# A decoder layer's down projection: four plain passes over the width, or seven of eight by Strassen's scheme

## The chip, the cores and the metric

One core of a Trainium2 chip runs the kernel once. The metric is the device time of one execution in microseconds (us); several executions give a median. The engines of the core are called by the profile's names: PE (TensorE, matmuls), PEld (its weight loads, which overlap the matmuls), DVE (VectorE), ACT (ScalarE), POOL (GpSimd) and SP (SyncE, which here issues nearly all DMAs).

## The reference

The layer has S = 512 tokens of width D = 1024; all data are float32. In short:

```python
a = rmsnorm(x, g_mix_pre);  z = a @ w_in
mix = concat(pool_mixer(z), moba_attention(z)) @ w_out
h = x + rmsnorm(mix, g_mix_post)
m = rmsnorm(h, g_mlp_pre)
f = square(relu(m @ w_up)) @ w_down          # w_up 1024x4096, w_down 4096x1024
h = h + rmsnorm(f, g_mlp_post)
out = h + sigmoid(h @ w_ple_gate) * (p @ w_ple_proj)
```

## The kernel before

Every product is made in three passes: each operand is split into a high part (rounded to the matmul's format by an ACT cast, line 123) and a low remainder (a DVE subtraction, line 124), and `three` (lines 158 to 160) multiplies high by high, high by low and low by high into one PSUM bank. A bank holds 128 rows of 512 columns; the program names eight: three `one`, three `four`, two `tp`.

Weights come in units of 128 x 1024 numbers (512 KB). `load` takes the next unit of a fixed list as soon as one of six slots is free: a DMA on SP into one of three `raw` buffers, the ACT cast, the DVE subtraction. `done` frees a slot behind the last matmul that reads it, so the list runs some five units ahead of PE. A planner puts each engine's instructions in an order ahead of the run, by program order and its own estimate of times; at run time each engine keeps that order.

The stages are: norm of x and the products with `w_in` and `w_ple_proj` (`embed(0, ...)` keeps the first half of the embedding's product in the tile `pp`); attention and pooling, head by head; the output projection in two halves `o0`, `o1` with both norms (`normed`), the second half of the embedding (`embed(1, ...)`) and the transposes of the normed rows (`mlp_rows`); the MLP; the gate.

The MLP goes over the 4096 in four chunks of 1024. In a chunk, `up` makes eight groups of 128 features for all 512 tokens (24 matmuls each), followed by relu (ACT), square (DVE), cast (ACT) and subtraction (DVE). The down products `tokens("d...")` take the two halves of the 1024 outputs in turn: the four token tiles fill four banks, and at a chunk's end ACT or DVE adds them to `facc` in SBUF. The last chunk goes half by half and tile by tile, with the norm's steps (lines 665 to 674), a transpose (`to_features`, line 238) and split of each finished tile behind its matmuls. The gate (lines 689 to 692) follows, tile by tile, in two halves.

The factor 2^-10 (`DOWN`) holds the rows that go into the MLP in range, whatever the gains; `squares` later takes it back out.

Of the kernel before, what the change touches and what calls it, by code (L numbers as in the profile page):

```python
# [25 lines left out]
NCH = 4  # L26
LINE = 512
FILL_LEFT, FILL_RIGHT = 192, 480
DOWN = 2.0 ** -10
# [13 lines left out]
def hybrid_layer(ctx: ExitStack, tc: tile.TileContext, x, p, w_in, w_pool, pool_scale, w_out,  # L43
# [68 lines left out]
    for c in range(NCH):  # L112
        for f in range(FC):
            rows(f"u{c}_{f}", w_up, 0, ND, (c * FC + f) * P, P)
        for hf in range(2):
            rows(f"d{c}_{hf}", w_down, c * FC, FC, hf * HALF, 512)
    for hf in range(2):
        rows(f"s{hf}", w_ple_gate, 0, ND, hf * HALF, 512)
# [10 lines left out]
    def load():  # L129
        while free and nxt[0] < len(units):  # L130
            i = nxt[0]
            nxt[0] += 1
            pool, s = free.pop(0)
            src, n, _ = units[i]
            raw = wts.tile([P, UD], F32, tag="raw", bufs=RAW, name="raw")
            hi = pool.tile([P, UD], F32R, tag=f"wh{s}", bufs=1, name=f"wh{s}")
            lo = pool.tile([P, UD], F32R, tag=f"wl{s}", bufs=1, name=f"wl{s}")
# [107 lines left out]
    pp = [keep.tile([P, NT, HALF], F32, name="pp0")]  # L245
    pT_h = keep.tile([P, NPK, S], F32R, name="pT_h")
    pT_l = keep.tile([P, NPK, S], F32R, name="pT_l")
# [43 lines left out]

    for t in range(NT):
        ms = small.tile([P, 1], F32, name="ms")
        an = begin.tile([P, D], F32, tag="an", bufs=2, name="an")
        with tc.issue_after(p_split.ins):
            mean_square(ms, xs[t], an)
        r = rstd(ms, eps)
        for hf in range(2):
            c = slice(hf * HALF, (hf + 1) * HALF)
            nc.vector.scalar_tensor_tensor(an[:, c], xs[t][:, c], r, gpre[:, c],  # L300
                                           op0=ALU.mult, op1=ALU.mult)
            to_features(an[:, c], aT_h, aT_l, t, 4 * hf, 4 * hf + 4)

    def embed(hf, bank, ts):
        for t in ts:
            o = bank()
            marks = tokens(f"e{hf}", pT_h, pT_l, [t], [o], t == NT - 1)
            (nc.scalar.copy if hf else nc.vector.tensor_copy)(pp[hf][:, t, :], o)
        return marks[-1]
# [224 lines left out]
    pp.append(mlp.tile([P, NT, HALF], F32, name="pp1"))  # L534
# [5 lines left out]
    def junk(n):  # L540
        return mlp.tile([P, n], F32, tag="rq", bufs=4, name="junk")
# [16 lines left out]

    def normed(t, o):
# [7 lines left out]
        for c in (LO, HI):  # L567
            last = nc.vector.scalar_tensor_tensor(m[:, c], h[:, c], DOWN, gmlp[:, c],
                                                  op0=ALU.mult, op1=ALU.mult)
# [29 lines left out]

    ypool.release()  # L600
    late = ctx.enter_context(tc.tile_pool(name="late", bufs=1, side="right", reuse_waits="tile"))
    fs = [small.tile([P, 2], F32, name="fs") for _ in ts]

    def up(c, f, fh, fl, cols=slice(0, S), last=True):
        n = cols.stop - cols.start
        o = one()[:, :n]
        mm = features(f"u{c}_{f}", mT_h, mT_l, o, cols, last)
        r = mlp.tile([P, n], F32, tag="rq", bufs=4, name="r")
        q = mlp.tile([P, n], F32, tag="rq", bufs=4, name="q")
# [5 lines left out]
    squares = []  # L615
    for c in range(NCH):
        if c == 1:
            table(AF.Sigmoid, facc[:, 0, 0:1])
        fh = late.tile([P, FC, S], F32R, tag="fh", bufs=1, name="fh")
        fl = late.tile([P, FC, S], F32R, tag="fl", bufs=1, name="fl")  # L620
        ahead = AHEAD if c == 0 else 0
        for f in range(ahead):
            mm = up(c, f, fh, fl, slice(0, S // 2), False)
            if f == 0:
                with tc.high_priority(), tc.issue_after(mm):
                    mlp_rows(NT - 1)
                mid.release()
                end = ctx.enter_context(tc.tile_pool(name="end", bufs=1, reuse_waits="tile"))
                facc = end.tile([P, NT, D], F32, name="facc")
                gfin = spread(end, g_mlp_post, "gfin")  # L630
        for f in range(FC):
            up(c, f, fh, fl, slice(S // 2 if f < ahead else 0, S))
        if c == 0:
            for t in ts:
                ms = small.tile([P, 2], F32, name="ms2")
                for hf, cc in enumerate((LO, HI)):
                    with tc.issue_after(root):
                        mean_square(ms[:, hf:hf + 1], h_sb[:, t, cc], junk(HALF))
                with tc.issue_after(made_m):
                    nc.vector.tensor_scalar(ms[:, 1:2], ms[:, 1:2], EPS, None, op0=ALU.add)  # L640
                    r = rstd(ms[:, 0:1], ms[:, 1:2])
                    q = small.tile([P, 2], F32, name="r2", bufs=NT)
                    nc.vector.tensor_scalar(q[:, 0:1], r, r, DOWN ** -2, op0=ALU.mult, op1=ALU.mult)
                    nc.vector.tensor_scalar(q[:, 1:2], q[:, 0:1], isd, None, op0=ALU.mult)
                squares.append(q)
        for hf in range(2):
            cc = slice(hf * HALF, (hf + 1) * HALF)
            if c < NCH - 1:
                os = [four(), four(), four(), one()]
                tokens(f"d{c}_{hf}", fh, fl, ts, os, True)  # L650
                for t in ts:
                    if c == 0:
                        nc.scalar.copy(facc[:, t, cc], os[t])
                    else:
                        nc.vector.tensor_add(facc[:, t, cc], facc[:, t, cc], os[t])
                continue
            if hf == 0:
                hT_h = act.tile([P, ND, S], F32R, tag="aTh", name="hT_h")
                hT_l = act.tile([P, ND, S], F32R, tag="aTl", name="hT_l")
            for t in ts:  # L660
                o = four()
                tokens(f"d{c}_{hf}", fh, fl, [t], [o], t == NT - 1)
                with tc.high_priority():
                    d, h = facc[:, t, :], h_sb[:, t, :]
                    nc.vector.tensor_add(d[:, cc], d[:, cc], o)
                    mean_square(fs[t][:, hf:hf + 1], d[:, cc], junk(HALF), squares[t][:, 1:2])
                    nc.vector.tensor_mul(d[:, cc], d[:, cc], gfin[:, cc])
                    if hf == 0:
                        nc.vector.tensor_scalar(fs[t][:, 0:1], fs[t][:, 0:1], EPS, None, op0=ALU.add)
                        continue  # L670
                    r = rstd(fs[t][:, 1:2], fs[t][:, 0:1], squares[t][:, 0:1])
                    for b in range(2):
                        bb = slice(b * HALF, (b + 1) * HALF)
                        nc.vector.scalar_tensor_tensor(h[:, bb], d[:, bb], r, h[:, bb],
                                                       op0=ALU.mult, op1=ALU.add)
                        to_features(h[:, bb], hT_h, hT_l, t, 4 * b, 4 * b + 4)
# [3 lines left out]
    for hf in range(2):  # L680
        for t in ts:
            tail = hf == 1 and t == NT - 1
            for c0, n in ((0, HALF // 2), (HALF // 2, HALF // 2)) if tail else ((0, HALF),):
                cc = slice(hf * HALF + c0, hf * HALF + c0 + n)
                o = four()[:, :n]
                tokens(f"s{hf}", hT_h, hT_l, [t], [o], t == NT - 1 and c0 + n == HALF,
                       slice(c0, c0 + n))
                g = mlp.tile([P, n], F32, tag="rq", bufs=4, name="g")
                nc.scalar.activation(g, o, AF.Sigmoid)
                nc.vector.tensor_mul(g, g, pp[hf][:, t, c0:c0 + n])  # L690
                nc.vector.tensor_add(g, g, h_sb[:, t, cc])
                nc.sync.dma_start(ot[t][:, cc], g)

# [28 lines left out]
```

## Time and profile before

| what | value |
|---|---|
| median of 3 executions (lowest, highest) | 602.88 us (602.8, 603.0) |
| the profiled execution's own time | 602.55 us |
| its span, first to last instruction | 600.8 us |
| busy: PE, DVE, ACT, POOL | 589.4, 320.3, 258.3, 53.3 us |
| granted clock of PE over the span | 0.999 |

Busy time counts the union of an engine's instructions. A matmul's end is modelled, so its listed length (0.39 us) is longer than the distance between two of them.

### The profile page before, as it was taken

Reading aid. Unit: us, or ns where it says so; the run is one execution under the profiler, and the core shown is the slowest. Engines: PE = TensorE matmul, PEld = TensorE weight load, DVE = VectorE, ACT = ScalarE, POOL = GpSimd, SP = SyncE. Lnnn points to the kernel's source line nnn. Section 1 sums busy time; section 2 is a strip of 40 time slices with the busy share of each in tenths; the row PEclk is TensorE's granted clock in tenths of the full one; section 3 lists DMA queues with packets and bytes.
Section 4 is the critical chain, followed back from the end, with each engine's and each line's share of the span. In section 5 each row is a group of like instructions: output and inputs, shape, how many; then the busy total and the mean of one; then the engine's idle time right before and its main releaser. Section 6 shows DMA issues by size and latency. Waiting matters only on the chain.

```text
span 600.8 us, 7438 instructions
## 1 busy us (share of the span) xinstructions
PE 589.4 (98%) x2854; PEld 492.5 (82%) x2854; DVE 320.3 (53%) x594; ACT 258.3 (43%) x447; POOL 53.3 (9%) x92
## 2 busy tenths in 40 slices
PE   8999999999999999999999999999999999999997
PEld 5678998987778998888888888888888888888886
DVE  5832788996558754622245334444244444368632
ACT  6554857676534544642434221343212343246221
POOL 2327363221000000000000000000000000000000
PEclk9999999999999999999999999999999999999999
DMA  8706431321390543233332233323323333043111
GB/s 313 218 16 175 116 109 57 97 79 36 93 328 1 174 141 106 73 107 100 106 105 90 86 106 105 95 83 104 105 76 102 104 106 103 3 140 99 43 54 52
DMA packets 65636, 63.16 MB, mean 105 GB/s; under 512 B 2356, under 2 KB 48184, under 8 KB 65600
## 3 DMA queue, kind: packets, MB, share of 16 engines
q1 hardware_dynamic: 65312, 61.90, 32.9%
q10 hardware_dynamic: 288, 0.79, 0.4%
q8 instruction: 22, 0.36, 0.2%
q14 instruction: 14, 0.11, 0.1%
HBM read 60.56 MB, written 2.12 MB: 104 GB/s over the span
## 4 chain that ended last, share of the span: by engine, by line
PE 88%; DVE 4%; ACT 3%; DMA 2%; issue 1%; POOL 0%; SPq 0%; ACTq 0%
PE ps_one L159 15%; PE ps_one L158 15%; PE ps_one L160 15%; PE ps_four L158 13%; PE ps_four L159 13%; PE ps_four L160 13%; ACT wh L123 1%; PE ps_tp L481 1%; PE ps_tp L238 1%; DMA raw<-in_w_ple_proj_dram 1%; PE ps_one L495 1%; DMA raw<-in_w_up_dram 1%; PE ps_one L496 1%; DVE wl L124 1%; PE ps_four L455 1%
## 5 line engine op out<-in xcount | busy, mean ns | idle before, releaser
L124 DVE TENSOR_TENSOR wl<-raw,wh 128x1024 fp32r<-128x1024 f32 (+1 forms) x87 | 105.1, 1211 | 163.0 <-ACT wh L123 162.4
L123 ACT CAST wh<-raw 128x1024 fp32r<-128x1024 f32 (+1 forms) x99 | 103.0, 1043 | 177.5 <-PE ps_one L160 79.0
L159 PE MATMUL ps_one<-mT_l,wh 128*128 128x512 f32 (+1 forms) x280 | 104.0, 372 | 0.4 <-DVE mT_l L124 0.4
L158 PE MATMUL ps_one<-mT_h,wh 128*128 128x512 f32 (+1 forms) x280 | 103.5, 371 | 0.0
L160 PE MATMUL ps_one<-mT_h,wl 128*128 128x512 f32 (+1 forms) x280 | 103.5, 371 | 0.0
L160 PE MATMUL ps_four<-wh,fl 128*128 128x512 f32 x208 | 81.0, 389 | 0.0
L158 PE MATMUL ps_four<-wh,fh 128*128 128x512 f32 x208 | 81.0, 389 | 0.0
L159 PE MATMUL ps_four<-wl,fh 128*128 128x512 f32 x208 | 80.9, 389 | 0.0
L159 PEld LDWEIGHTS ps_one<-mT_l,wh 128*128 128x128 f32 x280 | 52.7, 188 | 9.6 <-DVE mT_l L124 0.6
L158 PEld LDWEIGHTS ps_one<-mT_h,wh 128*128 128x128 f32 x280 | 52.6, 188 | 9.2
L160 PEld LDWEIGHTS ps_one<-mT_h,wl 128*128 128x128 f32 x280 | 52.6, 188 | 9.0
L158 PEld LDWEIGHTS ps_four<-wh,fh 128*128 128x128 f32 x208 | 39.0, 188 | 8.1
L160 PEld LDWEIGHTS ps_four<-wh,fl 128*128 128x128 f32 x208 | 39.0, 188 | 8.1
L159 PEld LDWEIGHTS ps_four<-wl,fh 128*128 128x128 f32 x208 | 39.0, 188 | 8.0
L158 PE MATMUL ps_one<-aT_h,wh 128*128 128x512 f32 (+1 forms) x120 | 42.3, 352 | 0.2 <-ACT ks L443 0.2
L160 PE MATMUL ps_one<-aT_h,wl 128*128 128x512 f32 (+1 forms) x120 | 41.9, 351 | 0.0
L159 PE MATMUL ps_one<-aT_l,wh 128*128 128x512 f32 (+1 forms) x120 | 41.9, 349 | 0.0
L123 ACT CAST fh<-q 128x512 fp32r<-128x512 f32 (+1 forms) x35 | 20.4, 583 | 41.9 <-DVE q L611 41.9
L124 DVE TENSOR_TENSOR fl<-q,fh 128x512 fp32r<-128x512 f32 (+1 forms) x35 | 22.6, 645 | 20.0 <-ACT fh L123 19.7
L124 POOL TENSOR_TENSOR wl<-raw,wh 128x1024 fp32r<-128x1024 f32 x12 | 28.7, 2400 | 29.7 <-ACT wh L123 29.6
L158 PE MATMUL ps_four<-wh,hT_h 128*128 128x512 f32 (+1 forms) x72 | 26.4, 367 | 0.0
L160 PE MATMUL ps_four<-wh,hT_l 128*128 128x512 f32 (+1 forms) x72 | 26.4, 368 | 0.0
(187 smaller groups left out, 934.7 us busy)
## 6 DMA issues: line engine op xcount, KB each, us to landing
raw<-in_w_up_dram SPq DMA_DIRECT2D x32, 512.0 KB, 3.8
raw<-in_w_down_dram SPq DMA_DIRECT2D x32, 512.0 KB, 3.7
raw<-in_w_in_dram SPq DMA_DIRECT2D x16, 512.0 KB, 4.1
raw<-in_w_out_dram SPq DMA_DIRECT2D x8, 512.0 KB, 3.7
raw<-in_w_ple_gate_dram SPq DMA_DIRECT2D x8, 512.0 KB, 4.6
T<-lines SPq DMA_DIRECT2D x8, 256.0 KB, 3.4
h_sb<-in_x_dram SPq DMA_DIRECT2D x4, 512.0 KB, 8.2
out_dram<-g SPq DMA_DIRECT2D x7, 256.0 KB, 2.0
```

The lines of the kernel that those rows point to most:

```text
L123: nc.scalar.copy(dst_hi, src)
L124: return (lo or nc.vector).tensor_tensor(dst_lo, src, f32(dst_hi), op=ALU.subtract)
L158: nc.tensor.matmul(o, sh, mh, start=start, stop=False)
L159: nc.tensor.matmul(o, sh, ml, start=False, stop=False)
L160: return nc.tensor.matmul(o, sl, mh, start=False, stop=stop)
L238: turned = nc.tensor.transpose(tp[:, k, :], src[:, (b - b0 + k) * P:(b - b0 + k + 1) * P], ident)
L455: nc.tensor.matmul(o[:, :wide], q[:, c], lo[:, :wide], start=False, stop=True)
L481: nc.tensor.transpose(tp[:, k, :], probs[t][:, k * P:(k + 1) * P], ident)
L495: nc.tensor.matmul(o[:, q0:], v, ph[:, c], start=k == 0, stop=False)
L496: nc.tensor.matmul(o[:, q0:], v, pl[:, c], start=False, stop=k == NT - 1)
```

## The change

The width is cut into eight chunks of 512 instead of four of 1024. In chunks 0 to 6 the down product of a chunk, 512 tokens by 512 features by 1024 outputs, is done by Strassen's scheme in Winograd's form: tokens, features and outputs are halved, and seven products of 256 x 256 x 512 take the place of eight. The seven stand in the order 1, 2, 6, 5, 7, 3, 4, with the next chunk's four `up` groups between them. Sums of the activations' quarters (`rows_of`: s1, s2, s3 and a fourth written over s2) and of the weights' quarters (`weights_of`: t1, t2, and two written in place) are DVE operations; each of the seven activations' and weights' operands is split into high and low. Products 2 and 4 stay in four PSUM banks over all seven chunks; the other five go through the two `tp` banks and are added in SBUF (`acc`) each chunk. At the end of chunk 6 five pairs of `acc` are combined (`add`). The weights' quarters are loaded whole (`fetch`, 512 KB each) and wait in `late`. The square of `up` moves from DVE to ACT, and the split of the hidden values moves to the quarters.

Chunk 7 is plain, and goes by token tiles with both halves of the outputs in turn; tiles 2 and 3 are transposed inside the gate's first matmuls (`turned_rows`).

The embedding's product goes to DRAM (`ppd`) through two small buffers and comes back before the gate. The factor 2^-10 becomes a factor per row worked out early from x and `g_mix_post` (`scale_of`, `size`); the table load ahead of chunk 1 is gone, and the scratch tiles `rq` have three buffers instead of four.

```diff
-NCH = 4
+NCH = 8
...
+            if callable(src):
+                src(hi, lo)
...
+            pp = keep.tile([P, HALF], F32, tag="pp", bufs=2, name="pp")
+            (nc.scalar.copy if hf else nc.vector.tensor_copy)(pp, o)
+            nc.sync.dma_start(ppd[hf, t], pp)
...
+    for hf, c in enumerate((LO, HI)):
+        mean_square(sq[:, hf:hf + 1], gpost[:, c], junk(HALF))
+    nc.vector.tensor_scalar(size, msx, sq[:, 0:1], sq[:, 1:2], op0=ALU.add, op1=ALU.add)
+    nc.scalar.activation(size, size, AF.Sqrt, bias=eps)
+    nc.vector.reciprocal(scale_of, size)
...
+    def weights_of(m, c):
+        def make(hi, lo):
+            b = {n: quads.get((n, c)) for n in ("11", "12", "21", "22")}
...
+            elif m == 6:
...
+                less(t1, b["12"], b["11"])
+                fetch("11", c + 1)
+                less(src, b["22"], t1)
+                fetch("21", c + 1)
...
+            elif m == 7:
+                src = b["12"]
+                less(src, b["22"], src)
...
+                src = b["21"]
+                less(src, src, quads["t2"])
+            split(hi, lo, flat(src))
+            if m in (7, 3):
+                fetch("12" if m == 7 else "22", c + 1)
...
+    order = [1, 2, "u0", 6, 5, "u1", 7, "u2", 3, "u3", 4]
...
         nc.scalar.activation(r, o, AF.Relu)
-        nc.vector.tensor_mul(q, r, r)
-        split(fh[:, f, cols], fl[:, f, cols], q)
+        nc.scalar.activation(qs_of[c][:, f, cols], r, AF.Square)
...
+        if m == 6:
+            nc.vector.tensor_add(tile("s1"), a["21"], a["22"])
+            less(tile("s2"), sums["s1"], a["11"])
+        elif m == 7:
+            less(tile("s3"), a["11"], a["21"])
+        elif m == 3:
+            less(sums["s2"], a["12"], sums["s2"])
...
+        split(hi, lo, src)
...
+    def product(m, c, i, o, start, stop):
...
+        for n in range(PAIRS):
+            three(o, sh[:, n, k], sl[:, n, k], wh[:, n, :], wl[:, n, :], start and n == 0,
+                  stop and n == PAIRS - 1)
...
+    held = {2: [four(), four()], 4: [four(), one()]}
+    def products(m, c):
+        for i in range(2):
+            if m in held:
+                product(m, c, i, held[m][i], c == 0, False)
+            else:
+                o = bank()
+                product(m, c, i, o, True, True)
+                if c == 0:
+                    nc.scalar.copy(acc[m][:, i, :], o)
+                else:
+                    nc.vector.tensor_add(acc[m][:, i, :], acc[m][:, i, :], o)
...
+    for c in range(NCH - 1):
+        for m in order:
+            if isinstance(m, str):
+                up(c + 1, int(m[1]))
                 continue
+            if k < len(line_up):
+                rows_of(*line_up[k])
+                k += 1
+            products(m, c)
...
+    for n in range(2 * NT):
+        nc.sync.dma_start(pp[n], ppd[n // NT, n % NT])
+    for t in ts:
+        mm = last_rows(t)
+        if t >= 2:
+            turned_rows(t - 2, mm)
...
+                if hf == 0 and t in (1, 2):
+                    turned_rows(t + 1, marks[1])
```

## Rows read from the trace of the kernel before

**Rows 1.** The page's first part and its chain: busy time of each engine, shares.

```profile
PE 589.4 (98%) x2854; PEld 492.5 (82%) x2854; DVE 320.3 (53%) x594; ACT 258.3 (43%) x447; POOL 53.3 (9%) x92
...
PE 88%; DVE 4%; ACT 3%; DMA 2%; issue 1%; POOL 0%; SPq 0%; ACTq 0%
```

**Rows 2.** Busy time by stretch: start, attention, before the MLP, steady MLP, end.

```profile
core 0: us, PE busy (x) PEld busy (x) DVE busy (x) ACT busy (x) POOL busy (x), PEclk, DMA share, GB/s
0.00:30.00 30.00, 25.73 (x105) 17.83 (x106) 21.73 (x47) 17.31 (x28) 8.52 (x44) 1.00 0.82 265
90.00:120.00 30.00, 29.81 (x184) 26.52 (x183) 27.03 (x72) 21.87 (x52) 9.43 (x16) 1.00 0.24 77
190.00:217.00 27.00, 26.60 (x198) 25.02 (x197) 19.82 (x33) 16.09 (x29) 0.00 (x0) 1.00 0.42 128
250.00:500.00 250.00, 250.00 (x1105) 207.01 (x1104) 98.61 (x133) 80.79 (x110) 0.00 (x0) 1.00 0.32 97
541.00:601.00 60.00, 55.52 (x284) 47.01 (x282) 32.06 (x55) 18.77 (x30) 0.00 (x0) 0.99 0.18 62
```

**Rows 3.** Groups by shape: line, engine, operation, count, busy, mean ns, idle before.

```profile
L124 DVE TENSOR_TENSOR wl<-raw,wh 128x1024 fp32r<-128x1024 f32 x85 | 103.8, 1224 | 157.7 <-ACT wh L123 157.1
L123 ACT CAST wh<-raw 128x1024 fp32r<-128x1024 f32 x97 | 101.8, 1052 | 174.4 <-PE ps_one L160 79.0 <-PE ps_one L159 67.5 <-PE ps_four L160 13.5
...
L158 PE MATMUL ps_four<-wh,fh 128*128 128x512 f32 x208 | 81.0, 389 | 0.0
...
L124 DVE TENSOR_TENSOR fl<-q,fh 128x512 fp32r<-128x512 f32 x29 | 20.1, 692 | 19.4 <-ACT fh L123 19.3
L611 DVE TENSOR_TENSOR q<-r 128x512 f32<-128x512 f32 x29 | 19.8, 684 | 0.0
...
L158 PE MATMUL ps_one<-wh,fh 128*128 128x512 f32 x48 | 18.7, 389 | 0.0
...
L123 ACT CAST fh<-q 128x512 fp32r<-128x512 f32 x29 | 18.0, 621 | 39.2 <-DVE q L611 39.2
L610 ACT ACTIVATE r<-ps_one 128x512 f32<-128x512 f32 x29 | 17.1, 591 | 0.0
...
L655 DVE TENSOR_TENSOR facc<-facc,ps_four 128x512 f32<-128x512 f32 x12 | 7.9, 682 | 2.3 <-PE ps_four L160 2.3
```

**Rows 4.** Timeline of DVE and ACT ahead of the MLP: start us, us, what.

```profile
189.54 1.28 DVE L124 TENSOR_TENSOR mT_l<-ps_tp,mT_h 128x512 fp32r<-128x512 f32 x2
...
198.01 3.48 DVE L124 TENSOR_TENSOR wl<-raw,wh 128x1024 fp32r<-128x1024 f32 x3
...
191.90 2.94 ACT L123 CAST wh<-raw 128x1024 fp32r<-128x1024 f32 x3
194.75 1.54 ACT L308 COPY pp<-ps_one 128x512 f32<-128x512 f32 x3
196.18 1.08 ACT L123 CAST mT_h<-ps_tp 128x512 fp32r<-128x512 f32 x2
```

**Rows 5.** Who waited for whom: total us, times, longest us.

```profile
DVE wl L124 <- ACT wh L123: 162.4, 66, 4.9
```

**Rows 6.** Timeline at a bank's release: DVE behind PE, PE behind DVE.

```profile
544.10 0.39 PE L160 MATMUL ps_four<-wh,fl 128*128 128x512 f32 x1
...
544.53 0.69 DVE L665 TENSOR_TENSOR facc<-facc,ps_four 128x512 f32<-128x512 f32 x1 [0.31 <-PE ps_four L160]
...
172.67 0.68 DVE L551 TENSOR_TENSOR mg<-ps_four,gpost 128x512 f32<-128x512 f32 x1
...
173.40 0.50 PE L158 MATMUL ps_four<-wh,Yh 128*128 128x512 f32 x1 [0.66 <-DVE ms L550]
```

**Rows 7.** Timeline of DVE and of SP's queue, 14 to 19 us.

```profile
14.18 1.28 DVE L308 COPY pp<-ps_four 128x512 f32<-128x512 f32 x2
15.38 1.22 DVE L124 TENSOR_TENSOR wl<-raw,wh 128x1024 fp32r<-128x1024 f32 x1
...
16.62 2.23 SPq L143 DMA_DIRECT2D raw<-in_w_in_dram  x2
```

**Rows 8.** DMA issues: count, KB each, median us from issue to landing.

```profile
h_sb<-in_x_dram SPq DMA_DIRECT2D x4, 512.0 KB, 8.2
out_dram<-g SPq DMA_DIRECT2D x7, 256.0 KB, 2.0
```

More of the change, by code (lines that the diff above doesn't have):

```diff
@@ L111, in hybrid_layer @@
     rows("e1", w_ple_proj, 0, NPK, HALF, 512)
[L112 to L118, printed above, removed]
+    for f in range(FC):
+        rows(f"u0_{f}", w_up, 0, ND, f * P, P)
     by_pool = set(range(groups["q0"][0], groups["o0"][0]))
@@ L134, in load @@
             src, n, _ = units[i]
+            if s == "q":
+                both = pool.tile([P, 2, UD], F32R, tag="q", bufs=2, name="wq")
+                hi, lo = both[:, 0], both[:, 1]
+            else:
+                hi = pool.tile([P, UD], F32R, tag=f"wh{s}", bufs=1, name=f"wh{s}")
+                lo = pool.tile([P, UD], F32R, tag=f"wl{s}", bufs=1, name=f"wl{s}")
+            if callable(src):
+                src(hi, lo)
+                loaded[i] = [t.rearrange("q (k c) -> q k c", k=n) for t in (hi, lo)] + [(pool, s)]
+                continue
             raw = wts.tile([P, UD], F32, tag="raw", bufs=RAW, name="raw")
-            hi = pool.tile([P, UD], F32R, tag=f"wh{s}", bufs=1, name=f"wh{s}")
-            lo = pool.tile([P, UD], F32R, tag=f"wl{s}", bufs=1, name=f"wl{s}")
             raw_k = raw.rearrange("q (k c) -> q k c", k=n)
@@ L244, in hybrid_layer @@
     keep = ctx.enter_context(tc.tile_pool(name="keep", bufs=1))
-    pp = [keep.tile([P, NT, HALF], F32, name="pp0")]
-    pT_h = keep.tile([P, NPK, S], F32R, name="pT_h")
-    pT_l = keep.tile([P, NPK, S], F32R, name="pT_l")
+    ppd = tc.dram_tile([2, NT, P, HALF], F32, name="ppd")
+    ppool = tc.alloc_tile_pool(name="ppool", bufs=1, side="right", reuse_waits="tile")
+    pT_h = ppool.tile([P, NPK, S], F32R, name="pT_h")
+    pT_l = ppool.tile([P, NPK, S], F32R, name="pT_l")
     aT_h = act.tile([P, ND, S], F32R, tag="aTh", name="aT_h")
@@ L290, in hybrid_layer @@
             nc.sync.dma_start(xs[t], xt[t])
+    msx = const.tile([P, NT], F32, name="msx")
     for t in range(NT):
-        ms = small.tile([P, 1], F32, name="ms")
+        ms = msx[:, t:t + 1]
         an = begin.tile([P, D], F32, tag="an", bufs=2, name="an")
@@ L540, in junk @@
     def junk(n):
-        return mlp.tile([P, n], F32, tag="rq", bufs=4, name="junk")
+        return mlp.tile([P, n], F32, tag="rq", bufs=3, name="junk")
     ts = list(range(NT))
@@ L600, in hybrid_layer, with fetch @@
     ypool.release()
-    late = ctx.enter_context(tc.tile_pool(name="late", bufs=1, side="right", reuse_waits="tile"))
-    fs = [small.tile([P, 2], F32, name="fs") for _ in ts]
-    def up(c, f, fh, fl, cols=slice(0, S), last=True):
+    ppool.release()
+    late = tc.alloc_tile_pool(name="late", bufs=1, side="right", reuse_waits="tile")
+    PAIRS = FC // 2
+    TH = S // 2
+    quads = {}
+    def fetch(name, c):
+        if c >= NCH - 1:
+            return
+        j, d = int(name[0]) - 1, int(name[1]) - 1
+        t = late.tile([P, PAIRS, HALF], F32, tag=f"b{name}", bufs=2 if name == "21" else 1,
+                      name=f"b{name}")
+        src = w_down[c * FC * P:(c + 1) * FC * P, d * HALF:(d + 1) * HALF]
+        nc.sync.dma_start(t, src.rearrange("(n j q) d -> j q n d", j=2, q=P)[j])
+        quads[name, c] = t
@@ L605, in up @@
+    order = [1, 2, "u0", 6, 5, "u1", 7, "u2", 3, "u3", 4]
+    qs_of, f7 = {}, []
+    def up(c, f, cols=slice(0, S), last=True):
         n = cols.stop - cols.start
+        if c not in qs_of:
+            qs_of[c] = late.tile([P, FC, S], F32, tag="q", bufs=2, name="q")
         o = one()[:, :n]
         mm = features(f"u{c}_{f}", mT_h, mT_l, o, cols, last)
-        r = mlp.tile([P, n], F32, tag="rq", bufs=4, name="r")
-        q = mlp.tile([P, n], F32, tag="rq", bufs=4, name="q")
+        r = mlp.tile([P, n], F32, tag="rq", bufs=3, name="r")
@@ L610, in up @@
         nc.scalar.activation(r, o, AF.Relu)
-        nc.vector.tensor_mul(q, r, r)
-        split(fh[:, f, cols], fl[:, f, cols], q)
-        return mm
[L615 to L630, printed above, removed]
-        for f in range(FC):
[L632 to L655, printed above, removed]
-                continue
[L657 to L676, printed above, removed]
@@ new lines, in up, with rows_of, tile @@
+        nc.scalar.activation(qs_of[c][:, f, cols], r, AF.Square)
+        if c == NCH - 1:
+            t = late.tile([P, 2, S], F32R, tag=("b21", "b11", "b12", "b22")[f],
+                          bufs=1 if f else 2, name="f7")
+            split(t[:, 0], t[:, 1], qs_of[c][:, f])
+            f7.append(t)
+        return mm
+    sums, parts = {}, {}
+    def rows_of(m, c):
+        v = qs_of[c].rearrange("q (n j) (i t) -> q i j n t", j=2, i=2)
+        a = {n: v[:, int(n[0]) - 1, int(n[1]) - 1] for n in ("11", "12", "21", "22")}
+        def tile(n):
+            sums[n] = late.tile([P, PAIRS, TH], F32, tag="s2" if n == "s2" else "s", name=n)
+            return sums[n]
+        if m == 6:
[3 more added lines that the diff above has]
+            less(tile("s3"), a["11"], a["21"])
+        elif m == 3:
+            less(sums["s2"], a["12"], sums["s2"])
+        src = {1: a["11"], 2: a["12"], 4: a["22"]}.get(m)
+        if src is None:
+            src = sums[{6: "s2", 5: "s1", 7: "s3", 3: "s2"}[m]]
+        hi = late.tile([P, PAIRS, TH], F32R, tag="sh", bufs=3, name="sh")
+        lo = late.tile([P, PAIRS, TH], F32R, tag="sl", bufs=3, name="sl")
+        split(hi, lo, src)
+        parts[m, c] = hi, lo
@@ new lines, in product, with bank @@
+    def product(m, c, i, o, start, stop):
+        sh, sl = parts[m, c]
+        wh, wl, _ = loaded[groups[f"w{c}_{m}"][0]]
+        k = slice(i * P, (i + 1) * P)
+        for n in range(PAIRS):
+            three(o, sh[:, n, k], sl[:, n, k], wh[:, n, :], wl[:, n, :], start and n == 0,
+                  stop and n == PAIRS - 1)
+    def bank():
+        return psum("tp", 2)
+    held = {2: [four(), four()], 4: [four(), one()]}
[3 more added lines that the diff above has]
+                product(m, c, i, held[m][i], c == 0, False)
+            else:
+                o = bank()
+                product(m, c, i, o, True, True)
+                if c == 0:
+                    nc.scalar.copy(acc[m][:, i, :], o)
+                else:
+                    nc.vector.tensor_add(acc[m][:, i, :], acc[m][:, i, :], o)
+        parts.pop((m, c))
+        done(groups[f"w{c}_{m}"][0])
@@ new lines, in hybrid_layer @@
+    for f in range(AHEAD):
+        mm = up(0, f, slice(0, TH), False)
+        if f == 0:
+            with tc.high_priority(), tc.issue_after(mm):
+                low = mlp_rows(NT - 1)
+    mid.release()
+    end = ctx.enter_context(tc.tile_pool(name="end", bufs=1, reuse_waits="tile"))
+    acc = {m: end.tile([P, 2, HALF], F32, name=f"acc{m}") for m in (1, 6, 5, 7, 3)}
+    gfin = spread(end, g_mlp_post, "gfin")
+    for c in range(NCH - 1):
+        for m in order:
+            if isinstance(m, str):
+                rows(f"u{c + 1}_{m[1]}", w_up, 0, ND, ((c + 1) * FC + int(m[1])) * P, P)
+            else:
+                groups[f"w{c}_{m}"] = [len(units)]
+                units.append((weights_of(m, c), PAIRS, 0))
@@ new lines, in hybrid_layer @@
+    for hf in range(2):
+        rows(f"d{hf}", w_down, (NCH - 1) * FC, FC, hf * HALF, 512)
+    for hf in range(2):
+        rows(f"s{hf}", w_ple_gate, 0, ND, hf * HALF, 512)
+    for name in ("11", "21", "12", "22"):
+        fetch(name, 0)
+    with tc.issue_after(low):
+        load()
+    with tc.issue_after(low):
+        for f in range(FC):
+            up(0, f, slice(TH if f < AHEAD else 0, S))
+    ms = small.tile([P, NT, 2], F32, name="ms2", bufs=1)
+    for t in ts:
+        for hf, c in enumerate((LO, HI)):
+            mean_square(ms[:, t, hf:hf + 1], h_sb[:, t, c], junk(HALF))
@@ new lines, in hybrid_layer @@
+    v, r, e, z2, z2d = (small.tile([P, NT], F32, name=f"z{n}", bufs=1) for n in range(5))
+    nc.vector.tensor_add(v, ms[:, :, 0], ms[:, :, 1])
+    nc.scalar.activation(e, v, AF.Sqrt, bias=eps)
+    nc.vector.tensor_scalar(v, v, EPS, None, op0=ALU.add)
+    nc.vector.reciprocal(r, e)
+    nc.vector.tensor_mul(e, r, r)
+    nc.vector.tensor_mul(e, e, v)
+    nc.vector.tensor_scalar(e, e, -0.5, 1.5, op0=ALU.mult, op1=ALU.add)
+    nc.vector.tensor_mul(r, r, e)
+    nc.vector.tensor_mul(r, r, size)
@@ new lines, in hybrid_layer, with add @@
+    nc.vector.tensor_mul(z2, r, r)
+    nc.vector.tensor_scalar(z2d, z2, isd, None, op0=ALU.mult)
+    line_up = [(m, c) for c in range(NCH - 1) for m in order if not isinstance(m, str)]
+    rows_of(*line_up[0])
+    rows_of(*line_up[1])
+    k = 2
+    def add(a, b):
+        for i in range(2):
+            nc.vector.tensor_add(acc[a][:, i, :], acc[a][:, i, :], acc[b][:, i, :])
+    for c in range(NCH - 1):
+        for m in order:
+            if isinstance(m, str):
+                up(c + 1, int(m[1]))
+                continue
+            if k < len(line_up):
+                rows_of(*line_up[k])
+                k += 1
+            products(m, c)
+            if c == NCH - 2:
+                if m == 5:
+                    add(6, 1)
+                elif m == 7:
+                    add(7, 6)
+                elif m == 3:
+                    add(3, 5)
+                    add(3, 6)
+                    add(5, 7)
@@ new lines, in hybrid_layer, with last_rows @@
+    free.append((late, "q"))
+    load()
+    hT_h = act.tile([P, ND, S], F32R, tag="aTh", name="hT_h")
+    hT_l = act.tile([P, ND, S], F32R, tag="aTl", name="hT_l")
+    roots = []
+    def last_rows(t):
+        i = t % 2
+        ds = [acc[m][:, i, :] for m in ((1, 3) if t < 2 else (7, 5))]
+        fs = small.tile([P, 2], F32, name="fs")
+        for hf, cc in enumerate((LO, HI)):
+            o = held[2 if t < 2 else 4][i] if hf == 0 else bank()
+            for j, u in enumerate(groups[f"d{hf}"]):
+                wh, wl, _ = loaded[u]
+                for k in range(2):
+                    f = 2 * j + k
+                    mm = three(o, f7[f][:, 0, t * P:(t + 1) * P], f7[f][:, 1, t * P:(t + 1) * P],
+                               wh[:, k, :], wl[:, k, :], hf == 1 and f == 0, f == FC - 1)
+                if t == NT - 1:
+                    done(u)
+            with tc.high_priority():
+                d = ds[hf]
+                nc.vector.tensor_add(d, d, o)
+                mean_square(fs[:, hf:hf + 1], d, junk(HALF), z2d[:, t:t + 1])
+                nc.vector.tensor_mul(d, d, gfin[:, cc])
+                if hf == 0:
+                    nc.vector.tensor_scalar(fs[:, 0:1], fs[:, 0:1], EPS, None, op0=ALU.add)
+        with tc.high_priority():
+            r = rstd(fs[:, 1:2], fs[:, 0:1], z2[:, t:t + 1], roots)
+            h = h_sb[:, t, :]
+            for b, cc in enumerate((LO, HI)):
+                nc.vector.scalar_tensor_tensor(h[:, cc], ds[b], r, h[:, cc], op0=ALU.mult,
+                                               op1=ALU.add)
+        return mm.ins
@@ new lines, in turned_rows @@
+    def turned_rows(t, after):
+        with tc.high_priority(), tc.issue_after(after):
+            to_features(h_sb[:, t, :], hT_h, hT_l, t, 0, ND)
+    tags = ["sh"] * 3 + ["sl"] * 3 + ["s", "s2"]
+    pp = [late.tile([P, HALF], F32, tag=tag, bufs=3 if len(tag) == 2 and tag != "s2" else 1,
+                    name="pp") for tag in tags]
+    for n in range(2 * NT):
+        nc.sync.dma_start(pp[n], ppd[n // NT, n % NT])
+    for t in ts:
+        mm = last_rows(t)
+        if t >= 2:
+            turned_rows(t - 2, mm)
@@ L685, in hybrid_layer @@
                 o = four()[:, :n]
[L686 to L690, printed above, removed]
+                marks = tokens(f"s{hf}", hT_h, hT_l, [t], [o], t == NT - 1 and c0 + n == HALF,
+                               slice(c0, c0 + n))
+                if hf == 0 and t in (1, 2):
+                    turned_rows(t + 1, marks[1])
+                g = mlp.tile([P, n], F32, tag="rq", bufs=3, name="g")
+                with tc.issue_after(roots[-1]):
+                    nc.scalar.activation(g, o, AF.Sigmoid)
+                nc.vector.tensor_mul(g, g, pp[hf * NT + t][:, c0:c0 + n])
                 nc.vector.tensor_add(g, g, h_sb[:, t, cc])
                 nc.sync.dma_start(ot[t][:, cc], g)
+    late.release()
 _INS = ['x', 'p', 'w_in', 'w_pool', 'pool_scale', 'w_out', 'rel_bias', 'g_mix_pre', 'g_mix_post',
```

27 lines of the change are left out of this document (21 added, 6 removed).

## The prediction

> **What bounds the kernel now.** I read the page's shares first. PE is busy for 589.4 of 600.8 us and the chain that ended last is 88% PE [rows 1]: the kernel is as long as its matmuls. The table by stretches then says where PE is not full. In the steady MLP it is busy in all of 250 us; it loses 4.3 us in the first 30, 0.4 us in the 27 ahead of the steady MLP, and what is missing behind 541 us is mostly the end of the program [rows 2]. So only fewer matmuls shorten the MLP, and only by what the other engines do not hand back as waits. In that stretch DVE is busy for 39% and ACT for 32%, at a granted clock of 1.00 (the 2.4 GHz level) and with DMA at a third [rows 2]. The big waits of DVE there, 162 us over the run for a weight's cast [rows 5], are no loss now: DVE has nothing else to do.
>
> One matmul of 512 columns costs 250 / 1105 = 0.2262 us [rows 2]; the listed 389 ns are a modelled length [rows 3]. Both forms, weights moving and activations moving, have the same length, so I use one price.
>
> **What is removed.** The down product now has (208 + 48) x 3 = 768 matmuls [rows 3]. After: 7 chunks x 7 products x 2 row tiles x 2 pairs x 3 passes = 588, and the plain chunk 4 tiles x 2 halves x 4 x 3 = 96; 684 in all. `up`, the embedding, the transposes and the gate keep their counts. 84 x 0.2262 = 19.0 us go. On this row the Trainium skill differs: "TensorE: Matmul & The Clock Gate", section "Wait — 56ns, not 53.3ns?", has 215.7 ns from start to start for 512 columns at the full clock, by which the saving would be 18.1 us; the row is 10.5 ns longer per matmul, and it decides.
>
> **What a chunk asks of the other engines.** PE needs (96 + 84) x 0.2262 = 40.7 us for a chunk of 512. For DVE I take distances between starts, since listed lengths overlap: three weight subtractions take 3.48 us with 1.224 each, so (3.48 - 1.224) / 2 = 1.13 us; two of 512 take 1.28, so 0.60 us [rows 3, 4]. Before, a chunk of 512 had 8 weight subtractions, 4 squares, 4 subtractions and 4 adds to `facc`: 8 x 1.13 + 12 x 0.60 = 16.2 us of 43.4, 37%, which agrees with the measured 39%. After: 11 weight subtractions and 4 sums of weight quarters (all 1024 wide; the sums are not in the trace, the subtraction is the nearest row) = 15 x 1.13 = 17.0; 7 subtractions of activations, 4 sums, 10 adds to `acc` = 21 x 0.60 = 12.6. That is 29.6 of 40.7 us, 73%. ACT: 11 casts at (2.94 - 1.052) / 2 = 0.94, and 4 relus, 4 squares and 7 casts, each 0.59 to 0.62 long and some 0.52 apart: 18.2 of 40.7 us [rows 3, 4]. DMA moves the same weights. So neither engine becomes the bound by its work alone.
>
> A rule speaks against this sum. The Trainium skill, "VectorE: DVE Perf Modes", section "The DRAIN you can't avoid", says that a DVE operation does not start until the one before has left the pipeline. By full lengths the load would be 15 x 1.224 + 21 x 0.684 = 32.7 us, 80%; the trace has the starts closer than the lengths, and even the rule's sum stays under PE's 40.7. By it the third rival below would decide with 10.3 us of casts exposed in a chunk instead of 13.4.
>
> **What the change may give back**, each from its nearest row, zero to the upper bound:
>
> The banks of products 6 and 5. Only here do two products that use the two `tp` banks stand back to back; elsewhere `up` or a product in its own banks lies between. A bank's add starts 0.43 us behind the start of its last matmul, takes 0.68, and PE follows 0.05 us later [rows 3, 6]: 1.16 us. PE fills the other bank for 6 matmuls and comes back after 7 x 0.2262 = 1.58. That leaves 0.42 us for whatever DVE is running. The average rest of a running operation is (17.0 x 0.56 + 12.6 x 0.30) / 40.7 = 0.33 us, the longest 1.13. So 0 to 0.7 us a chunk; I take 0.2, 7 x 0.2 = 1.4 us (0 to 4.9).
>
> The first product 2. Product 2 of chunk 0 needs features 1 and 3, thus the last `up` group: relu 0.59, square and cast 0.62 each, subtraction 0.69 = 2.52 us [rows 3] against 12 x 0.2262 = 2.71 us of product 1. In later chunks product 4 also lies between. One weight cast or subtraction ahead of it on ACT and DVE costs up to 2.2; I take 0.6.
>
> The embedding's stores. Four tiles pass two buffers, so the third copy waits for the first store to land: 2.0 us for 256 KB [rows 8]. At the start, the third copy would begin some 16.3 instead of 14.8 us; queued behind it on DVE stands the weight subtraction at 15.38, and behind that the next load on SP at 16.62, which PE is waiting for [rows 7]. The planner may put the copy later, at no cost; two copies in a row could cost 4.0. I take 0.5. Ahead of the MLP, ACT copies three tiles at 194.75 and then casts the rows that the MLP starts with [rows 4]; a store queued behind four loads of 512 KB (now `fetch`, once the attention's output is free) may take the 8.2 us of the `h_sb` loads [rows 8]. I take 0.6 (0 to 8.2).
>
> Early factor: two sums of squares of `g_mix_post` on ACT, some 0.6 each as the other 512-wide operations, and four small DVE operations, around 172 us, where PE waits 0.66 us for DVE already [rows 6]. Half of it can use ACT's idle time ahead; 0.2 (0 to 1.6).
>
> The end. In the last chunk DVE has, per tile, two adds, two products with the gain and two updates of `h_sb` plus the small steps of the norm, some 5 us at these prices, and two splits of transposed rows and three gate weights besides: 20 + 2.4 + 3.4 = 26 us against 96 x 0.2262 = 21.7 us of matmuls and two transposes. Its backlog can hold a `tp` bank or a split; a gate tile (24 matmuls, 5.4 us) then lies ahead of the next that is needed. I take 0.8 (0 to 4).
>
> Costed at nothing: the wait of the first sigmoid for the last square root (the gate's first tile covers it with 5.4 us), the square's move to ACT (45% busy), the loads of the embedding at the end (2 MB beside 6 MB of weights in over 60 us). If that cover went, a late sigmoid would hold one of three `four` banks only after 16 us.
>
> **Sum.** Against the profiled execution's own time: 602.55 - 19.0 + 1.4 + 0.6 + 0.5 + 0.6 + 0.2 + 0.8 = 587.65 us. The median lies 0.33 us above that execution, so 588.0 us. Range of this case alone: 584 to 593.
>
> **Rivals.** First, the order on DVE is worse than the average: each chunk's add of product 6 stands behind two 1024-wide operations instead of half of one. PE then waits 2 x 1.13 - 0.42 = 1.8 us a chunk, 12.9 in place of 1.4: 599.5 us. For it: DVE rises from 37% to 73%, and its order is fixed ahead. Against it: from 90 to 120 us, in the attention, DVE is busy for 90% and PE still for 99% [rows 2].
>
> Second, the stores bite at both ends of the embedding: 4.0 + 8.2 in place of 1.1: 599.1 us. For it: the start is the one stretch where PE already loses 4.3 us. Against: PE needs the copies only when it comes back to their banks, three products later, and 8.2 us is the time of four loads issued together.
>
> Third, the other side: casts exposed on DVE. Every subtraction needs its cast, and DVE waits for casts 66 times now, with 4.9 us the longest [rows 5]. With 11 weight casts of 1.05 and 7 of 0.62 a chunk all waited out in DVE's order, DVE needs 29.6 + 15.9 = 45.5 us against PE's 40.7: 7 x 4.8 = 33.6 in place of the 1.4 of banks: 620.2 us. It decides for slower once PE is held up by more than 19.0 - 2.7 = 16.3 us, 2.3 a chunk, that is with 13.4 of the 15.9 exposed (84%). Against it: five units ahead is some 18 us of lead, so most casts are done before DVE comes to them.
>
> **Chances.** Forecast 0.65; bad order on the banks 0.13; stores 0.10; exposed casts, or the milder ones together at the same price, 0.12. The measurement can tell about 0.2% from no change. The first three are all faster by over 0.2%; of the last I give 0.02 to a draw: faster 0.88, same 0.02, slower 0.10. For 8 in 10 the range goes from 583.5 (the saving with nothing given back, 602.88 - 19.0 = 583.9, and a little regained ahead of the MLP) to 598, into the first two rivals but not the third.
>
> **What the profile after should show.** PE with 684 down matmuls and the same distance of 0.226 us in the Strassen stretch; DVE near 73% and ACT near 45% busy there; small PE gaps only at product 5, released by a DVE add. PE waits of more than 1 us in every chunk would show the first rival; a later start of the steady MLP (217 us now) the second; PE waits released by weight or activation subtractions, with DVE waiting for casts in front, the third. I would be wrong if PE's distance were longer in the products, or if the last chunk's DVE backlog reached the gate in each tile.

## The result, and the profile after

The median went from 602.94 to 583.62 us (583.6 to 583.8); the ratio is 0.968, 95% interval 0.966 to 0.970. The profiled execution took 583.65 us, 18.9 less than the one before: of the 19.0 us of removed matmuls next to nothing came back.

Shares of the page and the table by stretches after, for [rows 1] and [rows 2]; the last row is the end, 16 us earlier at its start than in [rows 2]:

```profile
PE 570.5 (98%) x2770; PEld 476.4 (82%) x2770; DVE 416.2 (72%) x689; ACT 308.7 (53%) x522; POOL 55.5 (10%) x92
```

```profile
0.00:30.00 30.00, 26.36 (x112) 18.53 (x113) 21.73 (x47) 17.28 (x29) 10.66 (x44) 1.00 0.88 292
...
190.00:217.00 27.00, 26.34 (x197) 24.94 (x196) 21.89 (x29) 18.27 (x32) 0.00 (x0) 1.00 0.73 240
...
250.00:500.00 250.00, 250.00 (x1105) 207.01 (x1104) 188.88 (x220) 126.03 (x166) 0.00 (x0) 1.00 0.32 99
...
525.00:582.00 57.00, 52.19 (x268) 43.79 (x266) 30.40 (x53) 18.06 (x31) 0.00 (x0) 1.00 0.15 56
```

PE has 2770 instructions, 84 fewer. In the Strassen stretch it is full, with 1105 matmuls in 250 us as before: the same 0.2262 us each. DVE went from 39% to 76% there (73% forecast), ACT from 32% to 50% (45% forecast). The start lost 0.6 us less than before, the stretch ahead of the MLP and the end 0.3 more each.

What PE waits for, over the whole run, after (us in total, times, longest us); the two rows are what the change added:

```profile
PE ps_one L160 <- ACT pp L313: 0.7, 1, 0.7
...
PE ps_four L162 <- DVE hT_l L118: 0.3, 1, 0.3
```

The first is the store ahead of the MLP, the second the end. There is none at product 5. The timeline of PE says why: the last matmul of product 6 starts at 316.79 and the first of product 5 at 321.55, where the prediction had one directly behind the other (start, length, instruction; in brackets, where it has them, the idle time before and what ended it):

```profile
316.79 0.39 PE L162 MATMUL ps_tp<-wh,sl 128*128 128x512 f32 x1
317.01 0.39 PE L160 MATMUL ps_one<-mT_h,wh 128*128 128x512 f32 x1
...
321.32 0.39 PE L161 MATMUL ps_one<-mT_l,wh 128*128 128x512 f32 x1
321.55 0.39 PE L160 MATMUL ps_tp<-wh,sh 128*128 128x512 f32 x1
```

From 317.01 to 321.55 run (321.55 - 317.01) / 0.227 = 20 matmuls of the next chunk's `up`. The planner took them out of their written place and put them between the two products. The add of product 6 (0.68 us, as [rows 3] had it) is long done when its bank is wanted again.

### The profile page after: what moved, and what is told of

Same layout as the page of the kernel before. It is cut to its first block, busy times and chain, and to the rows that moved or that the text cites. A ratio compares the mean times of both kernels' runs of the same rounds, so it can differ in the third digit from the quotient of the medians.

```text
span 581.8 us, 7479 instructions
## 1 busy us (share of the span) xinstructions
PE 570.5 (98%) x2770; PEld 476.4 (82%) x2770; DVE 416.2 (72%) x689; ACT 308.7 (53%) x522; POOL 55.5 (10%) x92
## 4 chain that ended last, share of the span: by engine, by line
PE 87%; DVE 6%; ACT 3%; DMA 2%; issue 1%; POOL 0%; SPq 0%; ACTq 0%
PE ps_one L160 14%; PE ps_one L161 14%; PE ps_one L162 14%; PE ps_four L160 7%; PE ps_four L162 7%; PE ps_four L161 7%; PE ps_tp L161 6%; PE ps_tp L160 6%; PE ps_tp L162 6%; ACT wh L117 1%; PE ps_tp L487 1%; PE ps_tp L240 1%; DMA raw<-in_w_ple_proj_dram 1%; DVE wl L118 1%; PE ps_one L501 1%
## 5 line engine op out<-in xcount | busy, mean ns | idle before, releaser
L117 ACT CAST wh<-raw 128x1024 fp32r<-128x1024 f32 (+1 forms) x70 | 72.3, 1038 | 60.8 <-PE ps_four L162 23.7
L118 DVE TENSOR_TENSOR wl<-raw,wh 128x1024 fp32r<-128x1024 f32 (+1 forms) x58 | 69.5, 1202 | 25.7 <-ACT wh L117 25.1
L742 DVE TENSOR_TENSOR acc<-acc,ps_tp 128x512 f32<-128x512 f32 x60 | 41.1, 686 | 23.9 <-PE ps_tp L162 23.4
L160 PE MATMUL ps_tp<-wh,sh 128*128 128x512 f32 x140 | 54.5, 389 | 0.0
L161 PE MATMUL ps_tp<-wl,sh 128*128 128x512 f32 x140 | 54.5, 389 | 0.0
L162 PE MATMUL ps_tp<-wh,sl 128*128 128x512 f32 x140 | 54.5, 389 | 0.0
L117 ACT CAST wh<-b 128x1024 fp32r<-128x1024 f32 x35 | 36.3, 1051 | 27.7 <-PE ps_tp L162 15.6
L118 DVE TENSOR_TENSOR wl<-b,wh 128x1024 fp32r<-128x1024 f32 x35 | 42.3, 1222 | 8.6 <-ACT wh L117 8.0
L162 PEld LDWEIGHTS ps_tp<-wh,sl 128*128 128x128 f32 x140 | 26.3, 188 | 5.5
L160 PEld LDWEIGHTS ps_tp<-wh,sh 128*128 128x128 f32 x140 | 26.3, 188 | 5.5
```

What stands on the lines that cost most here:

```text
L117: nc.scalar.copy(dst_hi, src)
L118: return (lo or nc.vector).tensor_tensor(dst_lo, src, f32(dst_hi), op=ALU.subtract)
L160: nc.tensor.matmul(o, sh, mh, start=start, stop=False)
L161: nc.tensor.matmul(o, sh, ml, start=False, stop=False)
L162: return nc.tensor.matmul(o, sl, mh, start=False, stop=stop)
L742: nc.vector.tensor_add(acc[m][:, i, :], acc[m][:, i, :], o)
```

## The experiments

All are edits of the changed kernel; times are medians, to be held against 583.62 us.

**The matmuls back** (`mm84`). Product 7 twice:

```diff
-                product(m, c, i, o, True, True)
+                for _ in range(2 if m == 7 else 1):
+                    product(m, c, i, o, True, True)
```

> The changed kernel, with product 7 made twice into the same bank in each of the seven chunks, so that 84 matmuls come back and nothing else changes. Theory (the time is the number of matmuls times 0.2262 us, everything else is hidden): 583.6 + 19.0 = 602.6 us. Rival (VectorE or ScalarE paces the Strassen chunks and TensorE has hidden slack there): part of the 19.0 is swallowed, the time stays under 595 us.

603.09 us, 19.5 more, and next to the 602.64 of the kernel before in the same rounds: with its matmuls back, nothing is left of the gain. From the first product to the first matmul of chunk 7 PE takes 304.6 us, in the changed kernel 285.6: 19.0 more. TensorE has no hidden slack in the chunks.

**Half of product 7 left out** (`half7`).

```diff
-        for n in range(PAIRS):
+        pairs = 1 if m == 7 else PAIRS
+        for n in range(pairs):
...
-                  stop and n == PAIRS - 1)
+                  stop and n == pairs - 1)
```

> The changed kernel with half of the matmuls of product 7 left out (the second of its two pairs of feature blocks), 42 fewer over the seven chunks, all else kept; its output is that of a down projection without them. Theory (the number of matmuls sets the time, and VectorE has room for more savings, 29.6 us against 40.7 - 1.4): 583.6 - 9.5 = 574.1 us. Rival (with 181 us of 250 busy VectorE is already close behind, and a further saving comes back as waits): 578 us or more.

573.65 us, 10.0 less. The same stretch takes 276.1 us, 9.5 less, and the wait of 0.3 us at the end is not there. In both directions the count of matmuls sets the time.

**TensorE held to the written order**, in all chunks (`inorder`), in chunk 0 alone (`inorder0`), in chunks 1 to 6 alone (`inorder1`). Each block of PE's instructions is queued behind the last matmul of the block before:

```diff
...
             if isinstance(m, str):
-                up(c + 1, int(m[1]))
+                with prior:
+                    mm = up(c + 1, int(m[1]))
+                prior = tc.issue_after(mm)
                 continue
...
-            products(m, c)
+            with prior:
+                mm = products(m, c)
+            prior = tc.issue_after(mm)
```

> The changed kernel with TensorE held to the order that the program writes (1, 2, up 0, 6, 5, up 1, 7, up 2, 3, up 3, 4): products 6 and 5 stand back to back, where the planner had put 20 matmuls of up between them. Theory (the planner's order is why the term of the banks came out as nothing): the term of the prediction shows, 0.2 us a chunk, some 585.0 us (between 583.6 and 588.5), with TensorE waiting at product 5 for the add of product 6. Rival A (VectorE is free enough that the banks never bind): 583.6 us. Rival B (the adds stand behind two wide operations each): 596 us.

596.82 us: 13.2 more. The theory's number missed; the time is near rival B's figure, but not by its mechanism. The timeline of `inorder` has one long wait, at the first product 2, and ACT in front of it:

```profile
224.64 0.39 PE L162 MATMUL ps_tp<-wh,sl 128*128 128x512 f32 x1
229.71 0.50 PE L160 MATMUL ps_four<-wh,sh 128*128 128x512 f32 x1 [4.68 <-ACT sh L117]
...
231.09 0.63 PE L162 MATMUL ps_four<-wh,sl 128*128 128x512 f32 x1
231.52 0.63 PE L160 MATMUL ps_four<-wh,sh 128*128 128x512 f32 x1
```

```profile
227.01 0.57 ACT L741 COPY acc<-ps_tp 128x512 f32<-128x512 f32 x1
227.48 1.05 ACT L117 CAST wh<-b 128x1024 fp32r<-128x1024 f32 x1
228.42 0.63 ACT L212 ACTIVATE junk<-h_sb 128x512 f32<-128x512 f32 x1
228.96 0.19 ACT L212 ACTIVATION_READ_ACCUMULATOR junk<-h_sb 128x1 f32 x1
229.05 0.61 ACT L117 CAST sh<-q 128x512 fp32r<-128x512 f32 x1
```

The cast that product 2 needs (at 229.05) stands behind sums of squares of `h_sb`, copies and a weight cast. In the changed kernel it stands behind the same ones (at 228.72), but there 41 matmuls of `up` lie between products 1 and 2, and product 2 begins at 233.83 without a wait. Behind the wait the matmuls start 0.43 us apart, and the granted clock is 0.66 from 229 to 234 us: some eight matmuls at the 1.2 GHz level, 8 x 0.2 = 1.6 us more. At product 5 of each of the six later chunks PE loses 0.3 us at the first matmul and a little on the next, 0.4 in all: the add of product 6, 0.68 us, had begun behind a weight subtraction, as the prediction's term of the banks has it. At the end stand two waits of 1.2 and 1.4 us and seven matmuls 0.43 us apart, 1.4 us. Together 4.7 + 1.6 + 2.4 + 2.6 + 1.4 = 12.7 of the 13.6 us by which the profiled execution (597.27 us) is longer.

> The changed kernel with TensorE held to the program's order in chunk 0 alone. Theory (holding the order cost 13.2 us because of three places: 4.7 us of wait at the first product 2 and some 1.8 us of half clock behind it, 0.4 us at product 5 of each later chunk, and some 2.6 us at the end): the first part alone, 583.6 + 6.5 + 0.4 = 590.5 us. Rival (the wait at the first product 2 is made good later, for instance by weights that are further ahead then): 584 to 586 us.

> The changed kernel with TensorE held to the program's order in chunks 1 to 6 alone, free in chunk 0. Theory: six banks' waits of 0.4 to 0.5 us, 2.7 us, and the end's 2.6 us, 588.9 us. Rival (the end's waits do not come from the order): 586.3 us. Neither the wait at the first product 2 nor a fall of the clock there.

591.15 us for chunk 0 alone, 7.5 more where the theory had 6.9; the 4.7 us wait and the half clock are there again. 590.20 us (589.4 to 592.1) for chunks 1 to 6, 6.6 more where the theory had 5.3: six waits of 0.3 us at product 5, 1.2 and 1.4 us at the end, and, not counted in the theory, eight matmuls at half clock behind the last of these, 2.4 + 2.6 + 1.6 = 6.6.

**The copies free of the stores** (`rqpp`).

```diff
-            pp = keep.tile([P, HALF], F32, tag="pp", bufs=2, name="pp")
+            rq = hf == 1 and t >= 2
+            pp = (mlp if rq else keep).tile([P, HALF], F32, tag="rq" if rq else "pp",
+                                            bufs=3 if rq else 2, name="pp")
```

> The changed kernel, with the third and fourth tile of the second embedding stored from the scratch tiles rq instead of from the two small buffers, so that no copy waits for a store. Theory (the 0.66 us that TensorE waits at 197 us for a copy that waits for a store is the price of the stores ahead of the MLP): 582.9 to 583.1 us. Rival (another wait of the same stretch, a split of the normed rows or a weight, takes its place): 583.6 us.

583.51 us, no difference that can be told: the rival. PE still waits 0.4 us at that place for a copy that stands behind casts of the normed rows, and 1.0 instead of 0.7 us earlier, at the output projection.

**More work for VectorE.** The Strassen weights' subtraction three times in all (`dve14`), twice (`dve7`), twice in chunks 0 to 4 alone (`dve7early`). The edit of `dve14`; `dve7` has `range(1)`, and `dve7early` has `if c < 5:` in place of the loop:

```diff
             split(hi, lo, flat(src))
+            for _ in range(2):
+                nc.vector.tensor_tensor(lo, flat(src), f32(hi), op=ALU.subtract)
```

> The changed kernel, with the subtraction of each of the seven Strassen weights done three times instead of once (the same result), 14 more operations of 1.13 us a chunk on VectorE. Theory (VectorE needs 29.6 us a chunk by the sum over rows, so 45.4 with these, against 40.7 us of TensorE): 7 x 4.7 = 33 us more, some 617 us, VectorE nearly always busy in the Strassen stretch. Rival A (it needs more than the sum over rows, by the busy share of 77% after the change 31.4 us): 7 x 6.5 = 46 us more, some 629 us. Rival B (there is far more room than either): under 590 us.

616.38 us: the sum over rows. The stretch from 250 to 500 us, and the longest wait of PE:

```profile
250.00:500.00 250.00, 235.85 (x1004) 190.18 (x1003) 247.94 (x274) 113.33 (x152) 0.00 (x0) 0.98 0.28 87
...
PE ps_tp L240 <- DVE h_sb L856: 5.2, 1, 5.2
```

VectorE is full, and a chunk of 180 matmuls takes 180 x 250 / 1004 = 44.8 us (45.4 expected). For the first 50 us of this stretch TensorE is still full; over the other 200 it makes 790 matmuls, 45.6 us for 180. The wait of 5.2 us stands at the end, ahead of the gate, with VectorE busy in all of it: there the rest of its backlog comes out, and only with it does the loss reach the 33 us of the sum.

> The changed kernel, with the subtraction of each Strassen weight done twice, 7 more operations of 1.13 us a chunk on VectorE: 29.6 + 7.9 = 37.5 us by the sum over rows against 40.7 of TensorE. Theory (VectorE costs nothing until its sum passes TensorE's, as the run with 14 more operations fits): 583.6 us, at most 585. Rival (waits of VectorE for casts come on top, so that it binds earlier): 590 us or more.

588.59 us (586.6 to 590.1): the theory's number missed. But the chunks are not where it went:

```profile
250.00:500.00 250.00, 250.00 (x1105) 207.01 (x1104) 230.17 (x261) 125.46 (x167) 0.00 (x0) 1.00 0.31 97
```

VectorE is 92% busy and TensorE has all its 1105 matmuls. The loss is at the end. PE, then DVE, then the clock of `dve7` there:

```profile
529.18 0.40 PE L161 MATMUL ps_four<-wl,hT_h 128*128 128x512 f32 x1
531.84 0.79 PE L160 MATMUL ps_tp<-wh,f 128*128 128x512 f32 x1 [2.26 <-DVE hT_l L118]
532.43 0.63 PE L161 MATMUL ps_tp<-wl,f 128*128 128x512 f32 x1
```

```profile
528.17 1.22 DVE L118 TENSOR_TENSOR wl<-raw,wh 128x1024 fp32r<-128x1024 f32 x1
529.31 0.68 DVE L847 TENSOR_TENSOR acc<-acc,ps_one 128x512 f32<-128x512 f32 x1
529.90 0.16 DVE L224 RECIPROCAL rs_r<-rs_s 128x1 f32<-128x1 f32 x1
529.98 1.21 DVE L118 TENSOR_TENSOR wl<-raw,wh 128x1024 fp32r<-128x1024 f32 x1
531.10 1.28 DVE L118 TENSOR_TENSOR hT_l<-ps_tp,hT_h 128x512 fp32r<-128x512 f32 x2
```

```profile
531.00:536.00 5.00, 4.16 (x10) 3.29 (x11) 4.10 (x11) 1.04 (x1) 0.00 (x0) 0.50 0.58 196
```

The last token tile's second half wants a `tp` bank that holds transposed rows; their split waits on DVE behind two subtractions of gate weights. After the wait the clock is at 0.50 for twelve matmuls. With a wait of 0.7 us just ahead that is 0.7 + 2.3 + 12 x 0.2 = 5.4 of the 6.5 us by which the profiled execution (590.14 us, the slowest) is longer; 0.6 are lost ahead of the MLP, before the added work begins. VectorE's order at this place is not that of the changed kernel, where the first split stands ahead of both weights:

```profile
526.89 0.69 DVE L118 TENSOR_TENSOR hT_l<-ps_tp,hT_h 128x512 fp32r<-128x512 f32 x1
...
528.15 1.22 DVE L118 TENSOR_TENSOR wl<-raw,wh 128x1024 fp32r<-128x1024 f32 x1
...
529.47 1.22 DVE L118 TENSOR_TENSOR wl<-raw,wh 128x1024 fp32r<-128x1024 f32 x1
```

> The changed kernel, with the subtraction of each Strassen weight done twice in chunks 0 to 4 alone, so that VectorE is as full as in the run with 7 more operations (94% busy there, TensorE without a wait) until chunk 4, and as in the changed kernel from then on. Theory (that run's 5 us were lost at the end alone, in one wait of 2.3 us for a bank held by transposed rows and the half clock behind it; the load in the Strassen stretch itself costs nothing): 583.6 us, at most 584.5. Rival (the load costs time in the chunks, by a delay that the rows do not show as a wait): 586 to 588 us.

583.64 us. With the load in the early chunks alone (VectorE 217 of 250 us) nothing is lost, and the wait at the end is 0.3 us again.

**The square back on VectorE** (`sqdve`).

```diff
-        nc.scalar.activation(qs_of[c][:, f, cols], r, AF.Square)
+        nc.vector.tensor_mul(qs_of[c][:, f, cols], r, r)
```

> The changed kernel with one part undone: the square of the up product goes back from ScalarE to VectorE, 4 more operations of 0.60 us a chunk there (29.6 + 2.4 = 32.0 of 40.7 us), 4 fewer on ScalarE. Theory (moving it was not what made the time): 583.6 us, at most 585.5 if the order at the end falls differently. Rival (the square's place decides whether VectorE keeps up): 588 us or more.

586.76 us, 3.1 more, above the theory's bound. The chunks are full here too (1105 matmuls in the same 250 us); one wait of 1.7 us at the end for the same split, another of 0.4 just ahead of it, and eight matmuls at half clock behind, 1.6 us.

**Five weight slots** (`more1`: `MORE = 1` in place of 2):

> The changed kernel with five weight slots instead of six, so that the list runs four units ahead instead of five. Theory (the lead of some 18 us is more than the weights need, and the third rival of the prediction was far off): 583.6 to 585 us. Rival (the lead is what hides the casts): a wait at several products of each chunk, 590 us or more.

585.10 us. The chunks keep their 1105 matmuls; the 1.5 us are one more wait of that kind at the end, this time without a fall of the clock.

## Why the prediction was right, and where it was off

**What is removed**: 19.0 us, right, and bounded from both sides by the two runs that put matmuls back or leave more out. That VectorE at 73% is no bound held too: it binds where the sum over rows says, between a busy share of 92% (chunks untouched) and the sum of 45.4 us a chunk. With every operation held until the full listed length of the one before is over, that would be 29 x 1.224 + 21 x 0.684 = 49.9 us; the measured 44.8 to 45.6 is on the rows' side. The prediction took this rule from the Trainium skill ("VectorE: DVE Perf Modes", section "The DRAIN you can't avoid") without what that section adds to it, that a next operation which is not held starts earlier. The trace agrees with the addition: three weight subtractions of 1.224 us start 1.13 us apart [rows 4].

**What the change may give back** is the step that was off: 4.1 us were taken, 0.1 measured, so the forecast of 588.0 lay 4.4 us too high. The median lies just outside the 584 to 593 of the forecast's own case, and only 0.1 us above the 583.5 at which the range for 8 in 10 begins. That bound stood for the saving with nothing given back, so the range covered what came; why nothing came back, the prediction did not foresee. Term by term:

- *Banks of products 6 and 5*, 1.4 us: nothing. "Only here do two products that use the two `tp` banks stand back to back" was read from the program's order, and the planner does not keep it. Where it is kept, the size was in its bounds: 0.4 us a chunk against 0.2 taken.
- *First product 2*, 0.6: nothing, again by the planner, which had matmuls of `up` to put in front. Where the order is kept it costs 4.7 us and half clock, far above my 2.2: I had not counted the eight sums of squares of `h_sb` that the change keeps at this place on ACT, five of which stand ahead of the cast.
- *Stores*, 1.1: a wait of 0.7 us shows, but with no copy behind a store the time does not change; the start loses less than before.
- *Early factor*, 0.2: nothing; PE waits 0.7 us at that place as it did before.
- *End*, 0.8 (0 to 4): 0.3 here. The mechanism was right: five edits lose 1.5 us (`more1`, without a fall of the clock) to 5.4 us (`dve7`, with it) there, by the very bank and backlog that the term names. The upper bound had left out the clock: `inorder1` with 4.2 us and `dve7` with 5.4 lie above it. That the changed kernel loses only 0.3 is in part luck of the order on VectorE. Apart from `dve14` with its long backlog, the traces fall into two groups. In the changed kernel and in `mm84`, `half7`, `rqpp`, `inorder0` and `dve7early`, the first split of transposed rows stands ahead of the gate's weights, and PE waits at most 0.6 us for one; in `more1` it stands behind one of them, in `inorder`, `inorder1`, `dve7` and `sqdve` behind two, and PE waits 1.4 to 2.3 us. `inorder1` adds no work to VectorE and pays it. No run changes that order alone, so a part of the load is not excluded: `dve7` with the added work up to chunk 6 pays, `dve7early` with it up to chunk 4 does not.

**The rivals.** The bad order did not come: the planner put other work between the two products, and even where the written order is kept PE loses 0.4 us a chunk there, not 1.8. The stores did not bite. The casts were not exposed: one slot less cost no matmul in the chunks.

Open stays why the start lost 0.6 us less, and what leads the planner to the one order at the end or the other.

## What to carry to other kernels

Price a removal by the measured distance between instructions, and the load that replaces it by the same distances on the other engines; here both sums came within a few per cent. Do not price a wait from the written order where a planner may fill the place with independent work: ask first whether such work exists. And look for the loss where a stage ends: with spare work at hand the chunks absorbed their delays, while at the end the like of them became a wait, and a wait of some 2 us there could cost twice its length through the clock.

## What the runs showed of the hardware

A wait of TensorE can cost more than itself. Behind one of 4.7 us, and behind some of 1.4 to 2.3 us that followed other short gaps, the granted clock stood at the 1.2 GHz level for 7 to 12 matmuls (0.43 instead of 0.227 us apart), 1.4 to 2.4 us more; in `dve14` it did so for five to seven behind four waits of 2.4 to 5.2 us. In `more1` a wait of 1.5 us left it alone.

That is also the likely reason why `dve7` spreads over 3.5 us between executions where the changed kernel spreads over 0.2. The mean granted clock of each execution goes with its time: in `dve7` 590.14 us at 0.994, 588.62 and 588.55 at 0.997, 586.58 at 0.999; in `sqdve` 587.75 and 587.53 at 0.997, 586.00 and 585.97 at 1.000. It is no proof: in the changed kernel 0.998 and 1.000 both took 583.6 us, and only one execution of each kernel has a trace that shows where the clock fell.
